# Sums of squares of the input on VectorE alone, last scalings from PSUM, a one-operation seed for the reciprocal root

## The chip, the cores and the metric

The kernel runs on one core of a Trainium2 chip. The metric is the device time of one execution in microseconds (us). In the profile PE is TensorE's matmul side, PEld its weight loads, DVE is VectorE, ACT is ScalarE, POOL is GpSimd, SP is SyncE, which issues most DMAs. A name with a q behind it (ACTq, SPq) is that engine's queue of instructions that are not counted as busy, such as DMA issues.

## The reference, cut to what matters

The model has two layers over 1024 tokens of width 1024. Layer 0 is an mLSTM mixer with a SwiGLU block behind it, layer 1 a chunked attention with a SwiGLU block behind it, and a last normalization ends it. Every block starts with the same normalization:

```python
def rmsnorm(x, g):
    x32 = x.astype(jnp.float32)
    y = x32 * lax.rsqrt(jnp.mean(x32 * x32, axis=-1, keepdims=True) + EPS) * g.astype(jnp.float32)
    return y.astype(x.dtype)
...
hn = rmsnorm(h, norm_mix_g[l])
if l < N_A_LAYERS:
    h = h + mlstm_mixer(hn, a_w_in[l], a_b_gate[l], a_g_head[l], a_w_out[l])
...
h = h + swiglu(rmsnorm(h, norm_ffn_g[l]), ffn_w_gate[l], ffn_w_up[l], ffn_w_down[l])
return rmsnorm(h, final_norm_g)
```

So sums of squares over the 1024 features and their reciprocal roots are formed for the input, ahead of each SwiGLU block, ahead of the attention and at the end. The mLSTM has one more per head.

## The kernel before

**Layout.** The features lie on the partitions, in 8 tiles of 128, and the 1024 tokens along the free dimension, in two halves of 512. Every float32 product is formed from two parts of each operand, a rounded high part (suffix `h`, made by an ACT copy) and the rest (suffix `l`, made by a subtraction on DVE or POOL), as three matmuls: high by high, low by high, high by low. `xa0h` to `xa7l` are the parts of the input; `wh_ak`, `wl_ak` and the like are those of a weight block.

**Normalization.** The products are taken of the unnormalized tiles; the factor per token is multiplied in afterwards. `Stats.add` squares a tile (ACT) into `q` and adds it to the running sum `s` (tile `n_s` at the start, `f_s`, `b_s`, `fin_s` later). `last` says from which tile on the addition is done by DVE; below it POOL does it. `finish_a` sums `s` over the partitions with matmuls by a column of ones (`n_ps`, `f_ps`, `fin_ps`) and calls `rsqrt`, which makes a first guess on the bits of the number and refines it three times by small DVE operations (`_i`, `_y`, `_t`). `finish_b` spreads the result over the partitions by matmuls into PSUM (`n_pb`, `f_pb`, `fin_pb`), and ACT copies it into SBUF (`n_rbc`, `f_rbc`, `fin_rbc`).

**The start.** x and the first weights are loaded; the parts xa are made; PE begins with the gate products (`gate_p`) and the projections `aq_p` and `ak_p`, of 48 matmuls each, then `pv`. The gates of the mLSTM need `n_rbc`.

**SwiGLU.** `gate_up` works through 22 units of seven products (lines 989 and around), whose sums c are put together by DVE and POOL from PSUM tiles a, b, c, d. The first two units are interleaved, and the sum of squares is finished among them. `down` (line 1264) streams the second weight.

**The end.** In layer 1 the last product is cut so that the first half of the tokens is finished early. `scale_out` is called for tokens 0 to 511, 512 to 767 and 768 to 1023: it finishes the sums, and multiplies the eight tiles `hr` by the gain and by `fin_rbc`. Tiles 0, 3 and 6 get the gain on ACT and the factor on POOL, the other five both on DVE (line 1189). Each tile is then stored by a DMA, even ones from ACT's queue, odd ones from SP's.

**Order.** A scheduler sets each engine's order from the program; every engine then takes its instructions in that order, so an instruction that waits holds all behind it. Buffers come from pools with a fixed count (raw weights 2, high and low parts 3 each, 512-wide temporaries `half` 6), and a load waits until its buffer is free.

Of the kernel before, what the change touches and what calls it, by code (L numbers as in the profile page):

```python
# [10 lines left out]
I32 = mybir.dt.int32  # L11
AF = mybir.ActivationFunctionType
ALU = mybir.AluOpType
# [27 lines left out]
def tile_trunk(  # L41
# [19 lines left out]
    nc = tc.nc  # L61
# [22 lines left out]
    def coret(name, dt=F32):  # L84
        return full("core", name, dt)
# [7 lines left out]
    def pjt(name):  # L93
        return pools["pj"].tile([P, HT], F32, tag="pj", name=name)
# [4 lines left out]
    def smallt(n, tag, name, dt=F32):  # L99
        return pools["small"].tile([P, n], dt, tag=f"{tag}{n}", name=name)  # L100
# [12 lines left out]
    G_MIX0, G_FFN0, G_KV, G_MIX1, G_FFN1, G_FIN, G_HEAD = range(7)  # L113

    def gcol(which, k):
        return vec[:, which * NK + k : which * NK + k + 1]

    def hs(h):
        return slice(h * HT, (h + 1) * HT)
# [154 lines left out]

    def rsqrt(v, n, name):

        ti = smallt(8, "rsi", f"{name}_i", I32)[:, 0:n]
        nc.vector.tensor_scalar(ti, v.bitcast(I32), 1, None, ALU.logical_shift_right)
        y = smallt(8, "rsy", f"{name}_y")[:, 0:n]
        nc.vector.tensor_scalar(y.bitcast(I32), ti, -1, 0x5F3759DF, ALU.mult, ALU.add)  # L280
        t = smallt(8, "rst", f"{name}_t")[:, 0:n]
        for _ in range(3):
            nc.vector.tensor_tensor(t, y, y, ALU.mult)
            nc.vector.scalar_tensor_tensor(t, t, -0.5, v, ALU.mult, ALU.mult)
            nc.vector.scalar_tensor_tensor(y, t, 1.5, y, ALU.add, ALU.mult)
        return y

    class Stats:
# [22 lines left out]
        def finish_a(self, cols=slice(0, T), pin=False):  # L311
            t0, nt = cols.start // P, (cols.stop - cols.start) // P
            ps = mxt(f"{self.name}_ps{t0}")
            for i in range(nt):
                c = t0 + i
                mm = nc.tensor.matmul(  # L316
                    ps[:, i : i + 1], self.s[:, c * P : (c + 1) * P], ones, start=True, stop=True
                )
                if pin:
                    tc.keep_in_program_order(mm)  # L320
            with tc.high_priority():
                v = smallt(8, "rsv", f"{self.name}_v{t0}")[:, 0:nt]
                nc.vector.tensor_scalar(v, ps[:, 0:nt], 1.0 / T, EPS, ALU.mult, ALU.add)
                return rsqrt(v, nt, f"{self.name}{t0}")

        def finish_b(self, r_tok, r_bc, cols=slice(0, T), pin=False):
            t0, nt = cols.start // P, (cols.stop - cols.start) // P
            for i0 in range(0, nt, 4):
                n = min(4, nt - i0)
                pb = (pjt if pin and i0 else mxt)(f"{self.name}_pb{t0 + i0}")  # L330
                for i in range(n):
                    mm = nc.tensor.matmul(  # L332
                        pb[:, i * P : (i + 1) * P],
                        r_tok[:, i0 + i : i0 + i + 1].to_broadcast([P, P]),
                        ident,
                        start=True,
                        stop=True,
                    )
                    if pin:
                        tc.keep_in_program_order(mm)  # L340
                nc.scalar.copy(r_bc[:, (t0 + i0) * P : (t0 + i0 + n) * P], pb[:, 0 : n * P])

        def finish(self, r_bc, cols=slice(0, T)):
            r_tok = self.finish_a(cols)
            self.finish_b(r_tok, r_bc, cols)
            return r_tok


# [31 lines left out]
    def mlstm():  # L380
# [9 lines left out]
        st = Stats("n0")  # L390
# [10 lines left out]
        xr = []  # L401
# [18 lines left out]
            xs.append((hi, lo))  # L420
        for k in range(NK):
            for h in range(2):
                st.add(xr[k][:, hs(h)], hs(h), last=4)
        psg = [pjt(f"gate_p{h}") for h in range(2)]
        for k in range(NK):
            for h in range(2):
# [13 lines left out]
        r_bc = coret("n0_rbc")  # L440
        r_tok = st.finish(r_bc)
# [157 lines left out]
        def mix(t, d, fill):  # L599
# [113 lines left out]
            def norm(h):  # L713
                nv = num[h][:, :, :, 0:A_DV]
                den = num[h][:, :, :, A_DV]
                em = gt[:, 4 * h : 4 * h + 4, 2, 2 * t : 2 * t + 2].rearrange("p c j -> p j c")

                def s8(name):
                    return smallt(8, name, f"{name}{t}{h}")

                def j2(ap):
                    return ap.rearrange("p (j c) -> p j c", j=2)

                rec, ss, vv = s8("rec"), s8("ss"), s8("vv")
                nc.vector.scalar_tensor_tensor(j2(rec), den, -1.0, den, ALU.mult, ALU.max)
                nc.vector.tensor_tensor(j2(rec), j2(rec), em, ALU.max)
                nc.vector.reciprocal(rec, rec)
                x = ext(f"hv{t}{h}").rearrange("p (j c d) -> p j c d", c=4, j=2)
                hv[h] = x
                nc.gpsimd.tensor_tensor(x, nv, nv, ALU.mult)  # L730
                nc.vector.tensor_reduce(j2(ss), x, AX.X, ALU.add)
                nc.vector.tensor_tensor(ss, ss, rec, ALU.mult)
                nc.vector.scalar_tensor_tensor(vv, ss, 1.0 / A_DV, rec, ALU.mult, ALU.mult)
                nc.vector.tensor_scalar(vv, vv, EPS, None, ALU.add)
                y = rsqrt(vv, 8, f"hn{t}{h}")
                nc.vector.tensor_tensor(y, y, rec, ALU.mult)
                nc.vector.tensor_tensor(
                    x, nv, j2(y).unsqueeze(3).to_broadcast([P, 2, 4, A_DV]), ALU.mult
                )
# [87 lines left out]
        st = Stats("f0")  # L827
# [280 lines left out]
    def down(layer, mixed, hid):  # L1108


        last = layer == 1
# [54 lines left out]
        h = []  # L1166
        v = {}
        st = Stats("fin" if last else "b")
# [11 lines left out]
        def scale_out(cols):  # L1180
            r = r_fin[0]
            st.finish(r, cols)
            for e in range(NK):
                s_ = h[e][:, cols]
                if e % 3 == 0:
                    nc.scalar.activation(s_, s_, AF.Copy, scale=gcol(G_FIN, e))
                    nc.gpsimd.tensor_tensor(s_, s_, r[:, cols], ALU.mult)
                else:
                    nc.vector.scalar_tensor_tensor(  # L1189
                        s_, s_, gcol(G_FIN, e), r[:, cols], ALU.mult, ALU.mult  # L1190
                    )
                (nc.sync if e % 2 else nc.scalar).dma_start(out[e][:, cols], s_)

# [47 lines left out]
        for m, (i, u, at) in enumerate(order):  # L1241
# [15 lines left out]
            n = HT // 2 if last and i == 6 else HT  # L1257
# [15 lines left out]
            if last and (i, u) == (5, 0):  # L1273
                r_fin.append(coret("fin_rbc"))
                scale_out(hs(0))
            if last and (i, u, at) in ((6, 0, 1), (6, NU - 1, 1)):
                c = HT if u == 0 else HT + n
                scale_out(slice(c, c + n))
# [3 lines left out]
    def ffn(layer, mixed, st):  # L1282
        psc = Scope(mx=1, pj=7)
        kept = gate_up(layer, mixed, st)
        psc.close()
        psc = Scope(mx=2, pj=6)
        res = down(layer, mixed, kept)
        psc.close()
        return res
# [4 lines left out]
    def attention(xs, st):  # L1294
# [230 lines left out]
        return mixed, st  # L1525

    mixed, st = mlstm()
    xb, st = ffn(0, mixed, st)
    wsc = wscope()
    second_first[0] = True  # L1530
    mixed, st = attention(xb, st)
# [94 lines left out]
```

## Time and profile before

| what | value |
|---|---|
| median of 3 runs | 2409.1 us (2408.44 to 2414.58) |
| profiled execution, its own time | 2409.2 us |
| its span (first to last instruction) | 2407.2 us |
| PE busy | 2328.3 us, 97% |
| DVE busy | 1708.5 us, 71% |
| POOL busy | 986.4 us, 41% |
| ACT busy | 974.3 us, 40% |
| mean granted TensorE clock | 0.985 of full speed |

The span leaves 2.0 us of the execution's own time outside. PE is busy nearly throughout, so time is to be found where PE waits, where its clock is granted at half, and ahead of its first and behind its last matmul.

### The profile page before, as it was taken

To read this page: it belongs to the slowest core of one execution; us is meant where nothing else is said; L and a number is where in the kernel's file an instruction comes from. 1 tells how busy PE (TensorE), PEld (TensorE's weight loads), DVE (VectorE), ACT (ScalarE), POOL (GpSimd) and SP (SyncE) were. 2 spreads that over 40 slices of the span, in tenths; PEclk is the share of its full clock that TensorE was granted. 3 is DMA by queue.
4 is the path that set the end of the run, shared out by engine and by line. 5 is a ranking of instruction groups with operands and counts; after the bars stand their busy time and mean duration, and the time that the engine had idled before them with its cause. 6 is when DMAs were issued, how large, how long until landed. Compare 5 with 4: busy or idle time off the path is not lost. (4 is left out here: it accounts for less than half of the span.)

```text
span 2407.2 us, 31213 instructions
## 1 busy us (share of the span) xinstructions
PE 2328.3 (97%) x11568; PEld 1928.0 (80%) x11568; DVE 1708.5 (71%) x2703; ACT 974.3 (40%) x1826; POOL 986.4 (41%) x632
## 2 busy tenths in 40 slices
PE   8999999988999999999999999999889999999997
PEld 6888887877888887888879797878768888887887
DVE  5543546787777766797377777787886777766887
ACT  5322222442323233444366656665533233234444
POOL 2000000366666663012564545320676766651043
PEclk9999999989999999999999999999989999999999
DMA  3110102223232226743111011021322222329532
GB/s 137 44 36 27 45 14 92 90 90 110 98 117 92 105 79 232 295 145 129 62 46 46 30 47 37 26 99 40 110 96 96 101 109 88 120 99 352 186 106 73
DMA packets 91592, 237.49 MB, mean 99 GB/s; under 512 B 10160, under 2 KB 12976, under 8 KB 91440
## 3 DMA queue, kind: packets, MB, share of 16 engines
q1 hardware_dynamic: 89712, 233.41, 27.7%
q8 instruction: 90, 1.47, 0.3%
q10 hardware_dynamic: 1728, 2.10, 0.2%
q14 instruction: 62, 0.51, 0.1%
HBM read 178.32 MB, written 57.15 MB: 98 GB/s over the span
## 5 line engine op out<-in xcount | busy, mean ns | idle before, releaser
L1264 PE MATMUL dn<-hc,wc 128*128 128x512 f32 (+1 forms) x1980 | 428.6, 378 | 2.9 <-DVE wc L175 2.8
L1264 PEld LDWEIGHTS dn<-hc,wc 128*128 128x128 f32 x1980 | 354.3, 188 | 75.9 <-DVE wc L175 4.5
L989 PE MATMUL c<-t,wc 128*128 128x512 f32 x1056 | 260.0, 396 | 17.1 <-DVE c L1062 17.1
L989 PE MATMUL a<-b,wc 128*128 128x512 f32 x1056 | 260.1, 396 | 6.7 <-ACT wc L965 4.1
L989 PEld LDWEIGHTS c<-t,wc 128*128 128x128 f32 x1056 | 201.1, 191 | 62.2 <-DVE c L1062 17.9
L989 PEld LDWEIGHTS a<-b,wc 128*128 128x128 f32 x1056 | 200.7, 190 | 53.0 <-ACT wc L965 5.0
L967 DVE TENSOR_TENSOR wc<-s,wc 128x512 fp32r<-128x512 f32 x170 | 187.1, 1102 | 68.5 <-ACT wc L965 67.3
L965 ACT CAST wc<-s 128x512 fp32r<-128x512 f32 x176 | 107.8, 619 | 196.6 <-PE d L989 117.7
L730 POOL TENSOR_TENSOR hv<-num 128x1024 f32<-128x1024 f32 x8 | 15.2, 1895 | 342.5 <-ACT num L706 342.5
L174 ACT CAST wc<-wd 128x512 fp32r<-128x512 f32 x168 | 89.0, 581 | 149.4 <-PE dn L1264 120.5
L989 PE MATMUL b<-t,wc 128*128 128x512 f32 x528 | 134.9, 406 | 7.0 <-DVE wc L967 7.0
L989 PE MATMUL d<-b,wc 128*128 128x512 f32 x528 | 131.4, 398 | 0.0
L965 ACT CAST wc<-wr 128x512 fp32r<-128x512 f32 x132 | 80.7, 617 | 120.5 <-PE a L989 37.8
L989 PE MATMUL d<-n,wc 128*128 128x512 f32 x528 | 128.2, 392 | 0.0
L967 DVE TENSOR_TENSOR wc<-wr,wc 128x512 fp32r<-128x512 f32 x126 | 117.0, 929 | 15.1 <-ACT wc L965 15.1
L989 PEld LDWEIGHTS b<-t,wc 128*128 128x128 f32 x528 | 103.1, 196 | 30.6 <-DVE wc L967 7.8
L175 DVE TENSOR_TENSOR wc<-wd,wc 128x512 fp32r<-128x512 f32 x168 | 120.1, 754 | 10.7 <-ACT wc L174 10.4
L175 DVE TENSOR_TENSOR hc<-hr,hc 128x512 fp32r<-128x512 f32 x154 | 106.4, 731 | 22.4 <-ACT hc L174 22.1
L1405 ACT ACTIVATE p<-p,mn 128x640 f32<-128x640 f32 (+4 forms) x128 | 89.2, 697 | 81.0 <-DVE mn L1394 74.3
L989 PEld LDWEIGHTS d<-b,wc 128*128 128x128 f32 x528 | 99.8, 189 | 24.3
L1022 POOL TENSOR_TENSOR c<-c,c 128x512 f32<-128x512 f32 x44 | 73.3, 1667 | 105.4 <-DVE c L1066 90.9
L989 PEld LDWEIGHTS d<-n,wc 128*128 128x128 f32 x528 | 99.0, 188 | 21.5
(809 smaller groups left out, 5737.1 us busy)
## 6 DMA issues: line engine op xcount, KB each, us to landing
wd<-in_w_down_dram SPq DMA_DIRECT2D x40, 704.0 KB, 6.4
wr<-in_w_gate_dram SPq DMA_DIRECT2D x44, 512.0 KB, 4.3
wr<-in_w_up_dram SPq DMA_DIRECT2D x44, 512.0 KB, 4.3
kb<-c SPq DMA_DIRECT2D x66, 256.0 KB, 2.3
kt<-t SPq DMA_DIRECT2D x66, 256.0 KB, 2.1
hr<-kb SPq DMA_DIRECT2D x66, 256.0 KB, 4.1
hr<-kt SPq DMA_DIRECT2D x66, 256.0 KB, 4.6
hd<-h SPq DMA_DIRECT2D x16, 512.0 KB, 2.8
```

Source lines behind the costliest of these rows:

```text
L174: nc.scalar.copy(hi, src)
L175: nc.vector.tensor_tensor(lo, src, hi, ALU.subtract)
L730: nc.gpsimd.tensor_tensor(x, nv, nv, ALU.mult)
L965: hi = nc.scalar.copy(t[:, 0:HT], src)
L967: eng.tensor_tensor(t[:, HT:T], src, t[:, 0:HT], ALU.subtract)
L989: nc.tensor.matmul(ps, a, b, start=(first and k == 0 and i == 0), stop=(k == len(xs) - 1 and i == 2), skip_group_check=True,)
L1022: nc.gpsimd.tensor_tensor(x, x, g, ALU.mult)
L1264: nc.tensor.matmul(ps, a, b, start=(k == 0 and j == 0), stop=(k == NP - 1 and j == 2))
L1405: nc.scalar.activation(p, p, AF.Exp, bias=mnv, scale=-1.0, accum_out=sm)
```

## The change

Three edits. The sums of squares of the input are added on DVE alone (`last=0`), where POOL added the tiles 1 to 3. `rsqrt` makes its first guess in one operation that takes the bits as a number, where it took a shift and then a subtraction. `scale_out` lets DVE read the factor from PSUM, gives DVE six of the eight tiles in place of five, and POOL two (0 and 4) in place of three, which still read the copy in SBUF.

```diff
     def rsqrt(v, n, name):
 
-        ti = smallt(8, "rsi", f"{name}_i", I32)[:, 0:n]
-        nc.vector.tensor_scalar(ti, v.bitcast(I32), 1, None, ALU.logical_shift_right)
         y = smallt(8, "rsy", f"{name}_y")[:, 0:n]
-        nc.vector.tensor_scalar(y.bitcast(I32), ti, -1, 0x5F3759DF, ALU.mult, ALU.add)
+        nc.vector.tensor_scalar(
+            y.bitcast(I32), v.bitcast(I32), -0.5, float(0x5F3759DF), ALU.mult, ALU.add
+        )
...
                 nc.scalar.copy(r_bc[:, (t0 + i0) * P : (t0 + i0 + n) * P], pb[:, 0 : n * P])
+            return pb
 
         def finish(self, r_bc, cols=slice(0, T)):
             r_tok = self.finish_a(cols)
-            self.finish_b(r_tok, r_bc, cols)
+            self.pb = self.finish_b(r_tok, r_bc, cols)
             return r_tok
...
         for k in range(NK):
             for h in range(2):
-                st.add(xr[k][:, hs(h)], hs(h), last=4)
+                st.add(xr[k][:, hs(h)], hs(h), last=0)
...
             st.finish(r, cols)
+            pb = st.pb[:, 0 : cols.stop - cols.start]
             for e in range(NK):
                 s_ = h[e][:, cols]
-                if e % 3 == 0:
+                if e % 4 == 0:
                     nc.scalar.activation(s_, s_, AF.Copy, scale=gcol(G_FIN, e))
                     nc.gpsimd.tensor_tensor(s_, s_, r[:, cols], ALU.mult)
                 else:
                     nc.vector.scalar_tensor_tensor(
-                        s_, s_, gcol(G_FIN, e), r[:, cols], ALU.mult, ALU.mult
+                        s_, s_, gcol(G_FIN, e), pb, ALU.mult, ALU.mult
                     )
```

The scheduler places more than the edited instructions anew. DVE at the start, before, behind the low parts of x; `n_q_0` and `n_q_512` are the squares of the two halves of a tile:

```order
L162 TENSOR_TENSOR wl_ak_311<-wr_ak_308,wh_ak_310 128x1024
L162 TENSOR_TENSOR wl_av_0_380<-wr_av_0_377,wh_av_0_379 128x1024
L309 TENSOR_TENSOR n_s<-n_s,n_q_0_193 128x512
L309 TENSOR_TENSOR n_s<-n_s,n_q_512_196 128x512
...
L309 TENSOR_TENSOR n_s<-n_s,n_q_512_214 128x512
L162 TENSOR_TENSOR wl_av_1_449<-wr_av_1_446,wh_av_1_448 128x1024
L323 TENSOR_SCALAR n_v_263<-n_ps_254 128x8
L278 TENSOR_SCALAR n_i<-n_v_263 128x8
```

The same place in the changed kernel (whose lines from 276 on have other numbers):

```order
L178 SCALAR_TENSOR_TENSOR xa7l<-x_132,packed,xa7h 128x1024
L309 TENSOR_TENSOR n_s<-n_s,n_q_0_175 128x512
L309 TENSOR_TENSOR n_s<-n_s,n_q_512_178 128x512
...
L309 TENSOR_TENSOR n_s<-n_s,n_q_512_214 128x512
L162 TENSOR_TENSOR wl_ak_309<-wr_ak_306,wh_ak_308 128x1024
L323 TENSOR_SCALAR n_v_263<-n_ps_254 128x8
L162 TENSOR_TENSOR wl_av_0_378<-wr_av_0_375,wh_av_0_377 128x1024
L278 TENSOR_SCALAR n_y<-n_v_263 128x8
```

There are now 14 additions in place of 8, they stand right behind the parts of x, and the low parts of the weights ak and av stand behind them, the second of these between `n_v` and the first guess.

PE at the start, before: 17 matmuls of `ak_p` stand ahead of the first sums, three between the two groups of sums, and 13 between these and the spreading:

```order
L204 MATMUL aq_p_346<-xa7l,wh_aq_116 128x512
L204 MATMUL ak_p_383<-xa0h,wh_ak_310 128x512
L204 MATMUL ak_p_383<-xa0h,wl_ak_311 128x512
...
L204 MATMUL ak_p_383<-xa5h,wl_ak_311 128x512
L316 MATMUL n_ps_254<-ones,n_s 128x1 x4
L204 MATMUL ak_p_383<-xa5l,wh_ak_310 128x512
...
L316 MATMUL n_ps_254<-ones,n_s 128x1 x4
...
L332 MATMUL n_pb_279<-packed,n_y 128x128 x4
L332 MATMUL n_pb_285<-packed,n_y 128x128 x4
L204 MATMUL ak_p_414<-xa3h,wh_ak_310 128x512
```

PE at the same place in the changed kernel:

```order
L204 MATMUL aq_p_344<-xa7l,wh_aq_116 128x512
L204 MATMUL ak_p_381<-xa0h,wh_ak_308 128x512
L204 MATMUL ak_p_412<-xa0h,wh_ak_308 128x512
L316 MATMUL n_ps_254<-ones,n_s 128x1 x8
L204 MATMUL ak_p_381<-xa0h,wl_ak_309 128x512
...
L204 MATMUL ak_p_381<-xa4h,wl_ak_309 128x512
L332 MATMUL n_pb_277<-packed,n_y 128x128 x4
L332 MATMUL n_pb_283<-packed,n_y 128x128 x4
L204 MATMUL ak_p_381<-xa4l,wh_ak_308 128x512
```

Two matmuls stand ahead of all the sums now, 13 between sums and spreading, and 33 of `ak_p` behind that.

ACT in the second call of `scale_out`, before; `wc` is the high part of the last weight block, `fin_q_768` a square for the last 256 tokens:

```order
L174 CAST wc_21094<-wd_20473 128x512
L341 COPY fin_rbc<-fin_pb_21026 128x256
L304 ACTIVATE fin_q_768_21091<-hr_1_19267 128x256
L174 CAST wc_21094<-wd_20473 128x512
L1192 DMA out_dram<-hr_0_19266 128x256
L1192 DMA out_dram<-hr_2_19268 128x256
L1192 DMA out_dram<-hr_4_19270 128x256
L1192 DMA out_dram<-hr_6_19272 128x256
L174 CAST wc_21094<-wd_20473 128x384
```

ACT at the same place in the changed kernel:

```order
L341 COPY fin_rbc<-fin_pb_20997 128x256
L174 CAST wc_21064<-wd_20449 128x512
L1194 DMA out_dram<-hr_0_19242 128x256
L1194 DMA out_dram<-hr_4_19246 128x256
L1194 DMA out_dram<-hr_2_19244 128x256
L304 ACTIVATE fin_q_768_21061<-hr_1_19243 128x256
L174 CAST wc_21064<-wd_20449 128x512
L1194 DMA out_dram<-hr_6_19248 128x256
L174 CAST wc_21064<-wd_20449 128x384
```

The copy moved ahead of the first part of the weight block, and the stores of tiles 0 and 4, which POOL makes, ahead of its second part. The last call of `scale_out` has the same order of stores: 0, 4, 2, 6 in ACT's queue.

## Rows read from the trace of the kernel before

**Rows 1.** Who waited for whom, PE, whole span: total us, times, longest.
```profile
PE c L989 <- DVE c L1062: 17.1, 2, 9.6
...
PE fin_pb L332 <- DVE fin_y L285: 2.9, 2, 2.5
...
PE b_ps L316 <- DVE b_s L309: 1.4, 1, 1.4
```

**Rows 2.** The same view for PE, 0 to 420 us, its only rows.
```profile
PE gate_p L428 <- ACT xa0h L177: 6.7, 2, 6.3
PE n_ps L316 <- DVE n_s L309: 2.4, 1, 2.4
```

**Rows 3.** Timeline 20 to 50 us: start, us, engine, what, [idle before, releaser].
```profile
20.85 1.28 DVE L178 SCALAR_TENSOR_TENSOR xa7l<-x,packed,xa7h 128x1024 fp32r<-128x1024 f32 x1
...
29.39 0.39 PE L204 MATMUL ak_p<-xa0h,wh_ak 128*128 128x512 f32 x1
30.33 5.98 DVE L309 TENSOR_TENSOR n_s<-n_s,n_q 128x512 f32<-128x512 f32 x8 [3.69 <-POOL n_s L309]
31.58 1.79 ACT L304 ACTIVATE n_q<-x 128x512 f32<-128x512 f32 x3 [0.62 <-POOL n_s L309]
35.85 1.02 PE L316 MATMUL n_ps<-ones,n_s 128*128 128x1 f32 x8 [2.41 <-DVE n_s L309]
36.23 1.21 DVE L162 TENSOR_TENSOR wl_av<-wr_av,wh_av 128x1024 fp32r<-128x1024 f32 x1
39.43 0.17 DVE L278 TENSOR_SCALAR n_i<-n_v 128x8 int32<-128x8 int32 x1
39.63 0.17 DVE L280 TENSOR_SCALAR n_y<-n_i 128x8 int32<-128x8 int32 x1
44.58 1.95 PE L332 MATMUL n_pb<-packed,n_y 128*128 128x128 f32 x16
49.82 0.28 PE L232 MATMUL pv<-wh_av,xa0h 128*128 128x256 f32 x1
```

**Rows 4.** Busy us (instructions) of PE, PEld, DVE, ACT, POOL; granted clock, DMA, by stretch.
```profile
33.00:37.00 4.00, 1.59 (x11) 1.19 (x11) 4.00 (x7) 1.30 (x2) 0.00 (x0) 1.00 0.00 0
37.00:45.00 8.00, 8.00 (x28) 6.67 (x28) 2.46 (x13) 0.00 (x0) 0.00 (x0) 0.57 0.20 67
60.00:400.00 340.00, 340.00 (x1963) 279.61 (x1963) 168.62 (x359) 85.98 (x123) 11.62 (x8) 1.00 0.13 44
1154.00:1160.00 6.00, 5.30 (x14) 3.70 (x14) 5.50 (x3) 1.16 (x2) 5.67 (x2) 0.50 0.28 87
```

**Rows 5.** Line 309 up to 60 us: nanoseconds min/median/max of one.
```profile
L309 DVE TENSOR_TENSOR n_s<-n_s,n_q x8: 678/679/1768, 30.3 to 35.6; 128x512 f32<-128x512 f32 x8
```

**Rows 6.** Timeline of DVE, 505 to 524 us, and of POOL there.
```profile
507.96 0.62 DVE L278 TENSOR_SCALAR f_i<-f_v 128x8 int32<-128x8 int32 x1
508.62 1.20 DVE L280 TENSOR_SCALAR f_y<-f_i 128x8 int32<-128x8 int32 x1
512.42 0.69 DVE L1057 TENSOR_TENSOR v<-b,cp 128x512 f32<-128x512 f32 x1 [0.64 <-PE b L989]
522.80 3.51 POOL L881 TENSOR_TENSOR t<-t,t 128x512 fp32r<-128x512 f32 x2 [1.89 <-DVE t L914]
523.37 0.67 DVE L1066 TENSOR_TENSOR c<-c,d 128x512 f32<-128x512 f32 x1
523.97 1.19 DVE L178 SCALAR_TENSOR_TENSOR b<-h,packed,b 128x512 fp32r<-128x512 f32 x1
```

**Rows 7.** Single lines: nanoseconds min/median/max; c, d and pt lie in PSUM.
```profile
L1066 DVE TENSOR_TENSOR c<-c,d x44: 673/686/687, 523.4 to 2165.4; 128x512 f32<-128x512 f32 x44
L746 DVE SCALAR_TENSOR_TENSOR hst<-pt,packed,o x16: 740/743/746, 177.0 to 440.3; 128x512 f32<-128x512 f32 x16
L178 DVE SCALAR_TENSOR_TENSOR b<-h,packed,b x24: 735/750/1778, 446.6 to 1758.2; 128x512 fp32r<-128x512 f32 x24
L1189 DVE SCALAR_TENSOR_TENSOR hr<-hr,packed,fin_rbc x15: 471/955/1882, 2342.8 to 2402.1; 128x256 f32<-128x256 f32 x10, 128x512 f32<-128x512 f32 x5
```

**Rows 8.** Timeline of the end.
```profile
2398.59 0.37 ACT L341 COPY fin_rbc<-fin_pb 128x256 f32<-128x256 f32 x1 [4.38 <-PE fin_pb L332]
2399.00 3.56 DVE L1189 SCALAR_TENSOR_TENSOR hr<-hr,packed,fin_rbc 128x256 f32<-128x256 f32 x5 [1.78 <-ACT fin_rbc L341]
2399.04 2.45 POOL L1187 TENSOR_TENSOR hr<-hr,fin_rbc 128x256 f32<-128x256 f32 x3 [10.24 <-ACT fin_rbc L341]
2399.79 3.05 ACTq L1192 DMA_DIRECT2D out_dram<-hr  x4
2400.07 3.20 SPq L1192 DMA_DIRECT2D out_dram<-hr  x4
```

## The prediction

> **What bounds the kernel now.** I read the waits of PE first. Over the whole span PE waits little: two long waits for DVE inside the SwiGLU stages (17.1 us together), a few about the final sums, and one for the sums of the attention's normalization [rows 1]. Up to 420 us there are only two, the one for the first tile and 2.4 us for the sums of squares of the input [rows 2]; from 60 to 400 us PE is busy every microsecond [rows 4]. So what is gained or lost at the start stays until the first SwiGLU stage, where everything depends on what PE made before, and moves with it. The reciprocal roots inside the mLSTM lie wholly under this full stretch: eight fewer small operations there are worth nothing unless PE begins to wait.
>
> Then the timeline of the start. PE comes to the sums with `ak_p` at 33.3, waits 2.41 us, and does them from 35.85 [rows 3]. What follows is as dear as the wait: in 33 to 37 us PE is busy for 1.59 of 4 us, and from 37 to 45 us the granted clock is 0.57 of full [rows 4]. [...] Last the end: a copy by ACT at 2398.59, five DVE and three POOL operations, and stores issued until 2403.27 by SP and 2402.84 by ACT [rows 8].
>
> **The start, worked out.** DVE is free at 20.85 + 1.28 = 22.1 us [rows 3]. The eight additions took 5.98 us, of which the first, held up, took 1.77 [rows 3, 5]; the other seven took (5.98 - 1.77)/7 = 0.60 each. Fourteen of them end at 22.1 + 14 x 0.60 = 30.5. ACT makes a square each 0.6 us (three in 1.79) [rows 3]; six lie ready in the six buffers before 22, so I let DVE set the pace. Before, the last addition ended at 36.3. The low part of ak, once 1.2 us as its twin at 36.23 [rows 3], stands behind the additions and is ready at 31.7.
>
> PE reaches `ak_p` at 29.39 as before, and its matmuls there come every (33.05 - 29.39)/16 = 0.229 us [rows 3]. Two of them end at 29.9. The first half of the sums is ready at about 30.0; a group of sums takes 1.02 us at full clock [rows 3], so both end at 32.0, by when the low part of ak is there. Thirteen `ak_p` matmuls take 3.0: 35.0. Meanwhile DVE takes `n_v`, the low part of av (1.2), and ten small operations of 0.20 us start to start (39.43 to 39.63) [rows 3]: 32.1 + 0.2 + 1.1 + 2.0 = 35.4. PE waits 0.4, spreads for 1.95, and does 33 matmuls in 7.5 us: `pv` begins at 45.1, where it began at 49.82 [rows 3]. **Start: -4.7 us**, if the clock stays full. PE's waits shrink from 2.4 to under 1 us, and the stretch at the lower level goes.
>
> Whether it goes is the open point. PE does nothing but the sums between 29.9 and 32.0, that is 2.1 us, where before there were 3.6, from 33.3 to 36.9 [rows 3]. At 1154 us the clock fell to 0.50 for at least 6 us behind a wait of 1.4 us and sums around it [rows 1, 4]. A lower stretch as long as before would leave 4.7 - 3.4 = 1.3 us of gain, half as long 3.0.
>
> Loads behind this: the low part of ak is done 7 us later than before, which gives back a raw buffer later, so the second part of av and the first of ao load later. They are wanted at `pv` from 45 us and at `ao_p` some 22 us later, so I count nothing. The gates start earlier by more than PE does, so they cost nothing either.
>
> **One operation less in each reciprocal root.** On a clear path it is worth the 0.20 us from start to start [rows 3]. In the SwiGLU stage the pair takes 0.62 and 1.20 us beside POOL [rows 6], so 0.2 to 0.6 goes, but DVE then waits 0.64 for PE's b [rows 6], which eats most of it. The scheduler also moves ACT's copies of `f_rbc`, one POOL difference and one POOL scaling earlier, one POOL split later. The work stays the same, and the end of this stretch is DVE's queue, which PE waits for twice [rows 1]. I take **-0.3 for each of the two stages, -0.6 together**. Bounds: -2 each, if the POOL difference (1.7 us, as a split in rows 6) falls wholly into a gap; +2 each, if it holds up DVE where it did not. The attention's root has work of PE over it: nothing.
>
> **The last scalings.** DVE no longer waits for ACT's copy. What does an operation cost that reads PSUM? Line 1189 takes 0.47 us alone and 0.96 in the middle of its cases, five in 3.56 us beside POOL's three [rows 7, 8]. With one input in PSUM it is otherwise: line 1066 never took over 0.69 us in 44 cases; at 523.37 it took 0.67 under a POOL split that ran from 522.80, and the next operation, from SBUF, took 1.19 [rows 6, 7]. So six from PSUM cost what five did undisturbed, 0.4 to 0.5 each: DVE starts at 2398.4 (0.2 ahead of where ACT's copy stood) and ends by 2401, where it ended at 2402.56.
>
> [...]
>
> But the stores decide the end, four for each queue, 0.8 us apart [rows 8]. SP's first comes after DVE's first operation: 2398.9 + 3.2 = 2402.1, 1.1 earlier. ACT's first waits for POOL's first tile, and POOL still waits for the copy: 2398.4 + 0.4 + 0.8 = 2399.6, and 3.05 later 2402.65. The last store is issued at 2402.65 where it was at 2403.27: -0.6. Against it, in the second call PE meets the spreading two matmuls earlier, while the root there is interleaved with three subtractions that stay: 0.1 us of PE. **End: -0.5.** Bounds: -1.1 (both queues move with SP) and +0.6 (ACT's stores, now ahead of the second part of the last weight block, hold PE up by a microsecond).
>
> **The sum.** -4.7 - 0.6 - 0.5 = -5.8 on the profiled execution's own 2409.2 us (span 2407.2 and 2.0 around it), which is 0.1 over the median: **2403.4 us**, -0.24%. A measurement of this kernel tells about 0.3%, 7.2 us, from no change.
>
> **Rivals.**
> - *The clock falls at the start all the same.* For it: 1154 us, above. Against it: the idle stretch is shorter by a third and split by sums. 1.7 to 3.4 us of the gain go: 2405.1 to 2406.8.
> - *The SwiGLU stages gain more.* For it: POOL stands idle there between its splits (1.89 us ahead of one) [rows 6], and each long wait of PE ends with a chain through DVE, POOL and ACT, into which the earlier copies reach. With 2 us each in place of 0.3: 2400.0.
> - *Slower: the moved POOL work lengthens those two waits.* POOL's last split (`t`) now stands behind a scaling that waits for the copies; if it comes over 2 us later than before, PE waits for it, and DVE's operations from SBUF meet POOL at other places. With 2 us more for each stage and 3.4 us of lower clock behind one, and the start left with 1.3: 2409.2 - 1.3 + 4 + 3.4 - 0.5 = 2414.8. It needs the start to fail as well; the stage must lose over 3 us in all to undo the start.
> - *The additions don't run at 0.60.* If ACT or the buffers set the pace at the 0.82 that the eight averaged, they end at 33.6, the low part of ak at 34.8, PE loses 3 us more and the clock falls: the start gains nothing, 2408.1.
>
> **Chances.** Forecast 45%, clock 25%, SwiGLU better 15%, slower 7%, slow additions 8%. Faster by over 0.3% (under 2401.9): most of the SwiGLU rival and a third of the forecast, whose own range is 2401 to 2405.5: 0.29. Slower by over 0.3%: the far end of the slower rival, 0.04. The rest, 0.67, is within. The range takes in the bounds of the stages below and the slow additions above: 2398.5 to 2409.
>
> **What would show it.** The start is right if the sums begin near 30 us, the low part of ak ends near 31.7, and `pv` begins near 45; the clock's part is the granted clock between 30 and 45 us. The SwiGLU term shows in the two waits for DVE's c (7.5 and 9.6 us). The end is right if line 1189's successor takes under 0.5 us beside POOL, SP's stores end over a microsecond earlier, and ACT's end last. I am wrong if a new wait of PE stands in the first 60 us, if PE waits for a weight in the last 25 us, or if the two SwiGLU waits move by over 3 us.

## The result and the profile after

The changed kernel takes **2427.3 us** (median of 4 runs, 2426.1 to 2428.3) against 2408.8 for the kernel before beside it: ratio 1.0078, 95% interval 1.0066 to 1.009. It is slower by 18.5 us where 5.8 of gain were forecast, and outside the range. The profiled execution took 2426.35 us, with a span of 2424.4. All times below are medians of the fast executions; one slow execution each of runs 4 and 14 (3486 and 3259 us, at a mean granted clock of 0.61 and 0.65) is left out, with which these two would be 2402.8 and 2398.5.

The table of engines on the profile's page and its row of granted clocks, after:

```profile
PE 2351.8 (97%) x11568; PEld 1931.5 (80%) x11568; DVE 1707.8 (70%) x2697; ACT 973.8 (40%) x1823; POOL 966.4 (40%) x623
...
PEclk9999999999999999999999999999999999999999
```

PE has the same 11,568 matmuls as before, and is busy 23.5 us longer. Its clock is not the reason: the mean grant rose from 0.985 to 0.989. Nor do new waits explain it. Waits of PE after, answering to [rows 1] (total us, times, longest):

```profile
PE c L990 <- DVE c L1063: 10.5, 2, 5.3
...
PE a L990 <- DVE b L178: 5.3, 2, 2.7
...
PE fin_pb L332 <- DVE fin_y L285: 2.7, 2, 2.3
...
PE b_ps L316 <- DVE b_s L309: 1.4, 1, 1.4
```

The two waits for c lost 6.6 us, and 5.3 came back as waits for b: together a little less waiting than before. The timeline of the start, answering to [rows 3]:

```profile
21.55 4.90 DVE L309 TENSOR_TENSOR n_s<-n_s,n_q 128x512 f32<-128x512 f32 x8
26.61 3.70 DVE L309 TENSOR_TENSOR n_s<-n_s,n_q 128x512 f32<-128x512 f32 x6 [0.16 <-ACT n_q L304]
30.23 1.22 DVE L162 TENSOR_TENSOR wl_ak<-wr_ak,wh_ak 128x1024 fp32r<-128x1024 f32 x1
30.60 1.84 PE L316 MATMUL n_ps<-ones,n_s 128*128 128x1 f32 x16
35.73 2.05 PE L332 MATMUL n_pb<-packed,n_y 128*128 128x128 f32 x16 [0.17 <-DVE n_y L285]
```

The sums begin at 30.60 where 35.85 stood, and the wait ahead of the spreading is 0.17 us. `pv` starts at 45.27, 4.55 earlier. The windows answer to [rows 4]:

```profile
33.00:37.00 4.00, 3.83 (x23) 3.01 (x22) 3.11 (x12) 1.12 (x2) 0.00 (x0) 1.00 0.69 224
37.00:45.00 8.00, 8.00 (x39) 6.64 (x39) 7.78 (x11) 1.10 (x2) 0.00 (x0) 1.00 0.22 71
60.00:400.00 340.00, 340.00 (x1929) 277.76 (x1928) 159.71 (x335) 85.23 (x122) 11.62 (x8) 1.00 0.14 44
```

The clock stays full from 33 to 45 us. The third line holds the clue: PE is busy for all 340 us at full clock, as before, but gets through 1,929 matmuls where it had got through 1,963. Part of this is only that PE is some 4.6 us further on in its work where the window begins, so that the window holds other matmuls (run 1 below shows how large a part); for the rest, each matmul takes a little longer, and busy time cannot show that. In the first SwiGLU stage of the kernel before, PE's timeline from 700 us, 12 matmuls to a row:

```profile
699.86 2.91 PE L989 MATMUL c<-t,wc 128*128 128x512 f32 x12
702.61 2.98 PE L989 MATMUL d<-b,wc 128*128 128x512 f32 x12
705.42 2.91 PE L989 MATMUL a<-b,wc 128*128 128x512 f32 x12
708.17 2.91 PE L989 MATMUL b<-t,wc 128*128 128x512 f32 x12
```

and of the changed kernel:

```profile
699.68 2.96 PE L990 MATMUL a<-b,wc 128*128 128x512 f32 x12
702.48 2.96 PE L990 MATMUL c<-t,wc 128*128 128x512 f32 x12
705.28 2.96 PE L990 MATMUL d<-b,wc 128*128 128x512 f32 x12
708.08 2.96 PE L990 MATMUL a<-b,wc 128*128 128x512 f32 x12
```

Read the starts: before, a row of 12 comes 2.75 us after the last one, only that behind `d<-b` 2.81; after, always 2.80. From all starts in the trace, matmuls that follow one another by 205 to 260 ns (some 7,800 pairs) stand 229.5 ns apart before and 232.4 after; I call this the **spacing** (the expectations below say 229.8 and 232.7, the means of pairs 215 to 250 ns apart). The first matmul of a stage, after against before, shows the lead going: -4.55 us at `pv`, -2.0 at the first `pt` (174 us), +0.6 at `wb_p` (440 us), +6.3 at the first `dn` of the first layer, +20.2 at the second layer's `fin_ps`.

The end, which answers to [rows 8]:

```profile
2417.45 0.37 ACT L341 COPY fin_rbc<-fin_pb 128x256 f32<-128x256 f32 x1 [4.72 <-PE fin_pb L332]
2417.86 2.44 DVE L1191 SCALAR_TENSOR_TENSOR hr<-hr,packed,fin_pb 128x256 f32<-128x256 f32 x6 [1.78 <-ACT fin_rbc L341]
2417.90 1.41 POOL L1189 TENSOR_TENSOR hr<-hr,fin_rbc 128x256 f32<-128x256 f32 x2 [9.90 <-ACT fin_rbc L341]
2418.36 2.38 SPq L1194 DMA_DIRECT2D out_dram<-hr  x4
2418.66 2.01 ACTq L1194 DMA_DIRECT2D out_dram<-hr  x4
```

From the start of ACT's copy to the end of the span it is 6.95 us, before 8.6.

### The profile page after: what moved, and what is told of

Read it like the earlier page. It is cut to its first block, busy times and chain, and to the rows that moved or that the text cites. A ratio compares the mean times of both kernels' runs of the same rounds, so it can differ in the third digit from the quotient of the medians.

```text
span 2424.4 us, 31200 instructions
## 1 busy us (share of the span) xinstructions
PE 2351.8 (97%) x11568; PEld 1931.5 (80%) x11568; DVE 1707.8 (70%) x2697; ACT 973.8 (40%) x1823; POOL 966.4 (40%) x623
## 5 line engine op out<-in xcount | busy, mean ns | idle before, releaser
L990 PE MATMUL a<-b,wc 128*128 128x512 f32 x1056 | 265.8, 400 | 12.7 <-DVE b L178 5.3
L990 PE MATMUL c<-t,wc 128*128 128x512 f32 x1056 | 267.3, 403 | 10.5 <-DVE c L1063 10.5
L968 DVE TENSOR_TENSOR wc<-wr,wc 128x512 fp32r<-128x512 f32 x126 | 116.8, 927 | 13.8 <-ACT wc L966 13.8
L175 DVE TENSOR_TENSOR hc<-hr,hc 128x512 fp32r<-128x512 f32 x154 | 104.6, 720 | 22.1 <-ACT hc L174 21.9
L1023 POOL TENSOR_TENSOR c<-c,c 128x512 f32<-128x512 f32 x44 | 74.1, 1683 | 115.0 <-DVE c L1067 96.7
```

Source lines behind the costliest of these rows:

```text
L175: nc.vector.tensor_tensor(lo, src, hi, ALU.subtract)
L968: eng.tensor_tensor(t[:, HT:T], src, t[:, 0:HT], ALU.subtract)
L990: nc.tensor.matmul(ps, a, b, start=(first and k == 0 and i == 0), stop=(k == len(xs) - 1 and i == 2), skip_group_check=True,)
L1023: nc.gpsimd.tensor_tensor(x, x, g, ALU.mult)
```

## The experiments

**Theory.** The seed's edit also drops a tile, `rsi`: 32 bytes a partition, two buffers. The pool `small` lies behind the 25 activation tiles (`core`) and ahead of all pools opened later, so in the built program the tiles behind it, the weights of the large stages among them, stand 64 bytes lower than before, while `core` stays. The address theory is that the spacing follows where the tiles stand. **Rival:** the instructions do it, by another order or by more work of VectorE and GpSimd beside PE.

**1. The change, addresses put back.**

```diff
-        y = smallt(8, "rsy", f"{name}_y")[:, 0:n]
+        y = smallt(16, "rsy", f"{name}_y")[:, 0:n]
```

> The changed kernel with y's tiles twice as wide, so that every SBUF tile opened behind the pool of small tiles stands 64 bytes higher, at the address it has in the kernel before; no instruction differs but in addresses. In the trace of the changed kernel two matmuls of 128x512 that follow one another closely (205 to 260 ns apart, some 7,600 of 11,568) stand 232.70 ns apart in the mean, before 229.78: 7,600 x 2.92 ns = 22.2 us. Address theory: the spacing returns to 229.8 ns and the time to 2427.3 - 22.2 = 2405, range 2402 to 2408, so a little faster than before. Instruction theory (the other order of the work on the engines, or VectorE and GpSimd at other places, slows the matmuls): spacing stays 232.7 ns, time 2425 to 2429.

Measured 2402.7 us, ratio 0.9984 (0.9974 to 0.9993), spacing 229.5 ns. The whole loss is gone with no instruction changed. PE's window from 60 to 400 us in this run:

```profile
60.00:400.00 340.00, 340.00 (x1944) 1.00 0.14 44
```

Its `pv` begins as early as the changed kernel's (44.8 us) and its spacing is that of before. So of the 34 matmuls missing in this window after the change, 19 are the shift of the work, and 15 are the spacing.

**2. The kernel before, its addresses moved.**

```diff
-        ti = smallt(8, "rsi", f"{name}_i", I32)[:, 0:n]
-        nc.vector.tensor_scalar(ti, v.bitcast(I32), 1, None, ALU.logical_shift_right)
         y = smallt(8, "rsy", f"{name}_y")[:, 0:n]
+        ti = y.bitcast(I32)
+        nc.vector.tensor_scalar(ti, v.bitcast(I32), 1, None, ALU.logical_shift_right)
```

> The kernel before with the same instructions in the same order; only the shifted integers are written into y's tile instead of a tile of their own, so that the pool of small tiles is 64 bytes shorter and all tiles behind it stand 64 bytes lower, as in the changed kernel. Address theory: spacing 232.7 ns, time 2408.8 + 22 = 2431, range 2427 to 2434. Instruction theory: spacing 229.8 ns, time as before, 2407 to 2411.

Measured 2431.4 us, ratio 1.0103 (1.0087 to 1.0118), spacing 232.4. PE's timeline has the changed kernel's 2.80 us a row:

```profile
2080.41 2.96 PE L989 MATMUL d<-n,wc 128*128 128x512 f32 x12
2083.21 2.96 PE L989 MATMUL a<-b,wc 128*128 128x512 f32 x12
```

The instruction theory falls with these two runs.

**3. All tiles higher by 64 bytes.**

```diff
+    const.tile([P, 16], F32, name="pad")
     base = Scope(core=25, small=2)
```

> The changed kernel with an unused 64-byte tile ahead of the first pool: the tiles behind the small ones (weights of the dense stages) stand where they stand before, but the core tiles (activations, the moving side) are 64 bytes higher too, so all distances between tiles are those of the changed kernel. Address theory, if the place of the weights alone counts: spacing 229.8 ns and 2405. Address theory, if the distance between weights and activations counts: spacing 232.7 ns and 2427. Instruction theory: 2427 as well, told apart by the run with the gap behind the core tiles.

Measured 2425.2 us, ratio 1.0078 (1.0062 to 1.0095), spacing 232.4. The weights stand where they stood before and the kernel is as slow as the changed one: it is not their place alone, since nearly all distances are those of the changed kernel. For the rest I take for each matmul the **distance**, address of its weights less address of its moving tile in a partition, from the built program. Before, 6,884 of the 7,900 matmuls of 512 columns have 192 modulo 512, after 128; the 528 of the seventh SwiGLU product (`d<-b`) have 96 and 32. (These 528 are the exception in run 3: their moving tiles come from the other end of SBUF and do not move, so they are at 96 again.)

**4. The squares alone.**

```diff
-                st.add(xr[k][:, hs(h)], hs(h), last=4)
+                st.add(xr[k][:, hs(h)], hs(h), last=0)
```

> The kernel before with only the squares of the input moved to VectorE, addresses untouched. By the forecast the first stage gives 4.7 us and all of it stays to the end: 2404, range 2402 to 2407, spacing 229.8 ns, and no stretch at half clock before 60 us. By the rival that the gain is lost again in the stage that follows (the changed kernel's lead of 4.55 us at its first value projection is 2.8 at its next and none at 420 us): 2407 to 2409. The address theory puts that loss down to the spacing, so it sides with 2404.

Measured 2402.1 us, ratio 0.9986 (0.9976 to 0.9996). Its lead is 5.2 us at `pv` and still 5.2 at `wb_p`: at an unchanged spacing what is gained at the start stays. One thing was not expected: in its profiled execution (2409.4 us, the longest of the nine) the second layer's `dn`, from about 2190 to 2330 us, has 233.3 ns with addresses as before, where the kernel before has 228.9.

**5 and 6. Other gaps behind the small tiles**, of 32 and 192 bytes:

```diff
-    base = Scope(core=25, small=2)
+    base = Scope(core=25, small=2, gap=1)
+    pools["gap"].tile([P, 8], F32, name="gap")
```

(48 elements for 192 bytes.)

> The changed kernel with an unused tile of 32 bytes between the small tiles and all pools behind them. Of the 7,900 matmuls of 512 columns, 6,884 then have their weights 32 bytes past a multiple of 128 from their moving tile (0 in the changed kernel, 64 before), and the 528 of the seventh product of the dense units (out d from b, 96 before, 32 in the changed kernel) come to 64. Theory that only a distance of 64 modulo 128 is fast: main spacing as the 189 at distance 32 in the trace before, 233.2 ns, the 528 at 229; in all 232.4 to 233.0 ns and 2424 to 2429 us. Theory that a distance of 0 alone is slow and any other fast: main spacing 229, time 2402 to 2406.

> The same with a tile of 192 bytes, so that weights stand 128 bytes higher than with the gap of 64 that gave 2402.7 us: the main distance is 64 modulo 128 as there, but 320 modulo 512, where before and the gap of 64 had 192. If what counts repeats every 128 bytes: spacing 229.5 ns, 2401 to 2405 us. If it repeats only after 256 or 512 bytes, as far as these two distances tell it: spacing 232 ns or more, 2420 to 2430 us.

Measured 2431.2 us, ratio 1.0102 (1.0088 to 1.0116), and 2426.4, ratio 1.0079 (1.0065 to 1.0093); spacing 232.8 and 232.6. My guess of 64 modulo 128 was wrong on both counts: at 64 the seventh product has 233.1 ns, at 320 the main part 233.2.

**7. All large matmuls at 192 modulo 256.** The gap of 64 bytes, and three more:

```diff
+            self.extra = Scope("right", rgap=1, xce=NK // 2)
+            pools["rgap"].tile([P, 24], F32, name=f"rgap{layer}")
...
+        sb = Scope(v=3, q2=4, agap=1, ex=6, half=6, bias=2)
+        pools["agap"].tile([P, 16], F32, name="agap")
...
+        cst_.tile([P, 24], F32, name="vgap")
```

> The changed kernel with the gap of 64 bytes and three more unused tiles of 64 to 96 bytes, which bring all matmuls of 512 columns to a distance of 64 modulo 128: the 528 of the seventh product (96 before, 234.5 ns), the 192 of the second half of the first stage's output projection (32, 233.2 ns), and in attention those at distance 0. Address theory: 528 x 5.6 = 3.0 us and 192 x 4.3 = 0.8 us less than with the gap of 64 alone, in attention between 0 and 2: 2402.7 - 3.8 = 2399, range 2396 to 2400. If those groups are slow for another reason than the distance: 2402 to 2404.

Measured 2400.9 us, ratio 0.9979 (0.9966 to 0.9992). The two SwiGLU stages, 229.75 ns before with their slow seventh product, now have 228.9 and 229.05. So the distance explains a slow group inside the kernel before too. The time fell by 1.8 us where 3.8 were expected; each interval is some 3 us wide to either side, so the two cannot be told apart.

**8. The change without the squares, at the old addresses**: the gap of 64 bytes, and `last=4` again.

> The changed kernel with the gap of 64 bytes and the squares of the input divided between the engines as before, so that of the change only the one-operation seed and the last scalings from PSUM are left, at the addresses of before. By the forecast -0.6 and -0.5 us against before: 2406.4 - 1.1 = 2405.3, range 2403 to 2407. If the two runs so far (the whole change at the old addresses 2402.7, the squares alone 2402.8) are to be taken at their word, these two edits are worth nothing together: 2406 to 2408.

Measured 2406.6 us, ratio 0.9994 (0.9985 to 1.0003): consistent with -1.1 and with nothing.

**9 to 12. What repeats, and where it is fast.** Run 9 adds the 64-byte tile of run 3 to the gap of 64; the others have gaps of 320, 384 and 256 bytes, edited as in 5.

> The changed kernel with the gap of 64 bytes and, ahead of the first pool, another unused 64 bytes: weights and moving tiles both 64 bytes higher than with the gap alone, the main distance 192 modulo 512 as before. If the distance decides, whatever the places: spacing 229.5 ns, time 2401 to 2406. If it takes weights at 64 and moving tiles at 384 modulo 512 as before: spacing 232 ns or more, 2422 to 2430 us.

> The changed kernel with a gap of 320 bytes: main distance 448 modulo 512, that is 192 modulo 256. If what counts repeats every 256 bytes: spacing 229.5 ns, 2401 to 2406 us. If 192 modulo 512 alone is fast, of the distances so far: 232.4 to 233.3 ns, 2424 to 2431 us.

> A gap of 384 bytes: main distance 0 modulo 512, the 528 of the seventh product at 416. By the theory that 192 modulo 512 alone is fast: 232.4 to 233.3 ns, 2424 to 2431 us; any value below 230 ns in either group speaks against it.

> A gap of 256 bytes: main distance 384 modulo 512, the 528 of the seventh product at 288. As with the gap of 384: 232.4 to 233.3 ns and 2424 to 2431 us if 192 modulo 512 alone is fast; below 230 ns if 384 is fast too.

Measured 2401.6 us (0.9979, 0.9967 to 0.9991), 2401.4 (0.9984, 0.9972 to 0.9996), 2398.2 (0.9975, 0.9963 to 0.9987) and 2426.8 (1.0091, 1.0066 to 1.0117). Run 9 shows that the distance decides, not the places. Run 10 speaks for a period of 256, and run 11 overthrows "192 alone is fast": at 0 the matmuls are faster still. Mean spacing by distance, SwiGLU and down projection of the first layer (420 to 1175 us; each kernel's main group or its seventh product; pairs in brackets):

| distance modulo 512 | modulo 256 | ns | kernels |
|---|---|---|---|
| 0, 256 | 0 | 227.1 (2,597), 226.8 (3,046) | runs 11, 13 |
| 192, 448 | 192 | 229.0 (2,570), 229.0 (2,574) | before, run 10 |
| 128, 384 | 128 | 232.9 (2,543), 232.9 (2,548) | after, run 12 |
| 64, 320 | 64 | 233.1 (264), 233.2 (2,537) | runs 5, 6 |
| 32, 288 | 32 | 233.3 (263), 233.2 (189, the output projection) | after, before |
| 160, 416 | 160 | 233.3 (2,540), 234.5 (264) | runs 5, 11 |
| 224 | 224 | 232.8 (264) | run 6 |
| 96, 352 | 96 | 234.6 (264), 234.4 (263) | before, run 10 |

**13 and 14. Both kernels with every large matmul at 0 modulo 256.** Tiles as in 7 without `agap`, with a gap of 128 bytes (64 in the kernel before) and 8 elements for `vgap`.

> The changed kernel with unused tiles of 128, 96 and 32 bytes, which bring the main distance, that of the seventh product and that of the first stage's output projection to 256 modulo 512. If what counts repeats every 256 bytes: spacing as with the gap of 384 bytes (227.1 ns in the dense stages), now in the 528 of the seventh product (234.5 there) and the 192 of the projection (233.3) too: 2398.2 - 528 x 7.4 ns - 192 x 6.2 ns = 2393, range 2390 to 2396. If it repeats every 512 bytes only: 232 ns or more and 2422 to 2430 us.

> The kernel before with unused tiles of 64, 96 and 32 bytes, which bring its large matmuls to the same distances. If the edits themselves are worth what the comparison at the old addresses gave (2406.4 - 2402.7 = 3.7 us): 2393 + 3.7 = 2397, range 2394 to 2400. By the sum of the forecast (-5.8): 2399. If the edits are worth nothing once the matmuls run faster: the same time as the changed kernel at these distances.

Measured **2392.6 us**, ratio 0.9941 (0.9929 to 0.9953), and 2397.9, ratio 0.9965 (0.9952 to 0.9978). PE in run 13, 2.72 us a row:

```profile
2083.71 2.88 PE L993 MATMUL b<-t,wc 128*128 128x512 f32 x12
2086.43 2.88 PE L993 MATMUL c<-t,wc 128*128 128x512 f32 x12
2089.15 2.88 PE L993 MATMUL d<-n,wc 128*128 128x512 f32 x12
```

The windows view of PE from 1900 to 2100 us (busy us, matmuls, granted clock, DMA share, GB/s) shows the same as a count, first before, then after, then run 13:

```profile
1900.00:2100.00 200.00, 200.00 (x872) 1.00 0.28 101
```

```profile
1900.00:2100.00 200.00, 200.00 (x859) 1.00 0.28 99
```

```profile
1900.00:2100.00 200.00, 200.00 (x884) 1.00 0.30 106
```

Each of the seven distances modulo 256 that were met in both halves of 512 has nearly the same spacing in both: six agree to 0.3 ns, the pair of 160 and 416 to 1.2 (the table). Run 13 beats both kernels. The edits alone, at equal distances, are worth 5.3 us here (14 against 13) and 3.6 at the old addresses (before against 1).

## Why the prediction was wrong

**The step that failed** is "One operation less in each reciprocal root": I priced the operation and not the tile that went with it. Its bounds of 2 us a stage hold no such term, and no rival had it: the slower rival gave POOL's moved work as its reason, and run 1 has that work in the same places and is fast. The term is some 7,300 x 3.0 ns = 22 us from pairs of large matmuls; the 256-column matmuls of the value projections add 1,536 x 3.5 ns = 5 us where PE sets the pace (115.4 ns apart before, 118.9 after). As a whole it is 18.5 + 3.6 = 22.1 us, from the changed kernel and run 1, each against the kernel before beside it; in run 2, which has it alone, it is 2431.4 - 2406.4 = 25.1 us.

**Its premise**, "from 60 to 400 us PE is busy every microsecond [rows 4]. So what is gained or lost at the start stays", held for waits and not for the rate: at the same start, the same 340 us hold 15 matmuls fewer (1,929 against run 1's 1,944), and 200 us of the second SwiGLU stage 13 fewer (the window rows beside run 13). With the rate kept (run 4) it is true to a tenth of a microsecond.

**The start** was right for the trace that it was worked out from: -4.7 forecast, -4.55 after, -5.0 in run 1, -5.2 in run 4; the 14 additions took 8.8 us (forecast 8.4), the low part of ak ended at 31.45, and the clock stayed full. But 3.4 us of this, (1 - 0.57) x 8 by [rows 4] and the figure that the forecast's rivals use, are the stretch at half clock (granted 0.50 from 38 to 44 us in the kernel before), and the old start does not have it in every execution. In runs 2 and 14, which keep the instructions and the order of before, the clock is full from 37 to 45 us; run 14:

```profile
PE n_ps L317 <- DVE n_s L310: 1.6, 1, 1.6
37.00:45.00 8.00, 8.00 (x49) 1.00 0.22 67
```

There PE's matmuls came 0.43 us apart until 16.0 us (run 14) and 15.9 (run 2), in the kernel before until 13.8. So PE came to the sums later and waited 1.6 and 1.0 us for them in place of 2.4, and `pv` began at 46.96 and 46.48. Run 13 leads run 14 at `pv` by 2.6 us only. Of the four profiled executions with the old start, two have the stretch (before and run 8), of the twelve with the new one none. That the forecast was met to 0.2 us is thus in part the luck of which execution was profiled.

**The SwiGLU stages**, -0.6: in run 8, the first matmul on c has a lead of 0.15 us (0.06 at `pv`), the second stage's sums `f_ps` are 0.5 late, and the last `fin_pb` group has a lead of 0.4. So -0.6 is neither shown nor refuted: it lies within this scatter. In the changed kernel the waits moved by over 3 us, from c to b, which the text had named as a sign of being wrong; but run 1 has the same waits (10.3 and 6.9 us) and is fast, so they are not the loss.

**The end**, -0.5, was too small, and one reason was wrong. DVE did not get ahead of ACT's copy: it started 0.04 us after the copy ended, as before, and the trace names the copy as its releaser; in the built program the first of the six scalings still carries a wait for that copy. The gain came from the operations, six in 2.44 us where five had taken 3.56, and from POOL's two in 1.41 for three in 2.45. From the copy's start, the last store was issued after 3.29 us, before 4.68, and the span ended 1.7 us sooner. The rows from which the text took that an operation from PSUM is not slowed beside POOL proved right for these six: 0.41 us start to start.

**The sum** of the terms forecast, without the addresses, is 2403.4, and run 1 took 2402.7. That the times agree so well is partly luck: the forecast starts from 2409.2, and the kernel before took 2406.4 beside run 1. The gain there is 3.6 us (1.7 to 6.3) where 5.8 were forecast. In the profiled executions it is 6.8, and there the one of before has the stretch at half clock. Whether the stretch accounts for the difference is not shown: of the executions that were not profiled no clock by stretch is known.

## What to carry to other kernels

An edit that frees or adds a tile moves every tile behind it, here by 64 bytes for a tile of 32 in two buffers; list which operands of the busiest engine move against which, and put a filler in the tile's place before the edit is judged. When PE is busy in every microsecond of a window, compare the number of matmuls in it, not the busy time, and take a window in which both kernels do the same kind of matmul. Before a stretch at half clock is counted as a gain, look whether other executions of the same code have it. Once the critical matmuls are known, try the distance between weights and moving tiles in steps of 32 bytes: here three unused tiles of 192 bytes in all gave the kernel before 8.7 us (run 14), more than the three edits.

## What was not expected of the hardware

Matmuls of 512 columns at full clock came 226.8 to 234.6 ns apart, by the distance between weights and moving tile modulo 256 bytes; 0 (226.8 and 227.1) and 192 (229.0) were fast, the other six multiples of 32 slow (232.8 to 234.6). Why is not settled; no run here takes one of the two operands away. That the place of tiles costs time at all is plainest in run 2: the same instructions, with the tiles behind the small ones 64 bytes lower, took 2431.4 us where the kernel before takes 2406.4.

The distance that is best for one kind of matmul is not best for another. The value projections, 256 columns with the activations as weights, came 115.4 ns apart before (64 modulo 256), 118.9 after (128) and 119.6 in run 13 (0): that version still loses there, and was not improved further. It seems to go with the number of columns rather than with what serves as weights: the 256-column matmuls of the last `dn`, which have the model's weights there, came 115.0 ns apart at 64 (run 6), 117.8 at 192 (before) and 119.9 at 0 (run 13). Nor is the spacing fixed by addresses alone: the one stage of run 4 at 233.3 ns stays unexplained, and in the attention's projections (`bk_p`, `bq_p`, `oa_p`), which other work interrupts, the same distances lie closer together: 230.0 ns at 0 (run 11), 230.4 to 230.9 at 192 (before), 232.1 to 232.3 at 128 (after), 233.6 to 233.9 at 160 (run 5).
